# Turned tiles of a hybrid encoder layer: written to DRAM in four parts and read back in one transfer

## The chip, the cores and the metric

The kernel runs on one core of one Trainium2 chip. The core has five engines that run side by side: TensorE (PE in the profile, with its weight loads as PEld), VectorE (DVE), ScalarE (ACT), GpSimd (POOL) and SyncE (SP), which only issues transfers here. Sixteen DMA engines move the data. The metric is the device time of one execution in microseconds (us), the median of several runs.

## The reference

One layer of a bidirectional encoder, with 512 tokens of width 2048, all in float32:

```python
def hybrid_layer(x, norm_w, w_in, ...):
    h = rms_norm(x, norm_w)
    proj = jnp.einsum('bsd,de->bse', h, w_in)
    q, k, v, g_attn, xr, g_lru = jnp.split(proj, SPLITS, axis=-1)
    attn_out = attention_group(q, k, v, q_norm_w, k_norm_w)
    lru_out = lru_group(xr, conv_w, conv_b, lru_wa, lru_ba, lru_wx, lru_bx, lru_lambda)
    mixed = jnp.concatenate([rms_norm(attn_out, attn_norm_w) * jax.nn.silu(g_attn),
                             rms_norm(lru_out, lru_norm_w) * jax.nn.silu(g_lru)], axis=-1)
    return x + jnp.einsum('bse,ed->bsd', mixed, w_out)
```

The attention has 8 heads of 128 on 2 key/value heads, with a norm and a rotary embedding on queries and keys and a softmax over all 512 tokens. The other branch is a short convolution with a gated linear recurrence in both directions. `w_in` is 2048 x 4608 and `w_out` 2048 x 2048.

## The kernel before

**Products in three matmuls.** A float32 product is made of three matmuls on rounded operands (`mm3`, L152): each operand is split into a high part (a copy that rounds) and a low part (the difference), and high x high, high x low and low x high are added. So each weight tile `wr` passes ScalarE (`wh`, L223) and VectorE (`wl`, L224) before TensorE can use it, and so do x, keys, queries and attention weights. Weights come in chunks of 256 rows by 512 columns, 512 KB each, through a ring of three places.

**Turning tiles.** TensorE needs several tiles with rows and columns exchanged. Three kinds are turned without TensorE: the last three of the eight chunks of x (`TURNED = 5`), the keys and queries, and the attention weights (the softmax result, called p). VectorE turns every 32 x 32 block in place (`blocks`, L284, and the transpose at L713). What then remains is to bring each block to its new group of 32 partitions (`B = 32`, four groups, `NQ = 4`). That goes through a buffer in DRAM: a write of the whole tile, 128 partitions with 4 KB each (`put_aside`, L291; the first lines of `moved`, L718), and four reads back, one for each group of 32 partitions, which pick four pieces of 1 KB for every partition (`bring_back`, L297; the loop in `moved`). All of these transfers are issued by SP. Each tile has a DRAM buffer to itself.

- x: `xchunk` (L308) for chunks 5, 6 and 7 loads, turns, puts aside (`xd`), brings back (`xu`), scales on ScalarE (L343) and splits (L344). The table `moves` (L1206) says at which step of the first projection each part is issued.
- Keys and queries: `sent` (L637) turns a pair of heads and puts it aside (`qd`), `landed` (L649) brings it back (`lq`), `split_head` (L655) splits it (L658). The keys are one tile, the queries four.
- Attention weights: `weights` (L698) makes p for one head and 128 queries and turns it. Two of these are a unit; `moved` (L718) writes a unit (`pd`, L721) and, when it is called again, reads it (`pt`, L728) and splits it on ScalarE (`ph`) and VectorE (`pl`, both L732). `values` (L735) multiplies with v once the two units of a head are there. In `attention` (L764) a unit is written one step after its second half was made and read two steps later, and the values of a head come `LATE = 3` steps after it (`BEGIN, STEPS, LATE = 11, 2, 3`).

**The order.** TensorE's order is written by hand for the whole program (L1160): the matmuls of one projection are woven with the small products of the stage before. SP's order is written by hand in the first projection (L1172 to L1245), in the attention stage (L1340) and in the last stage. ScalarE and VectorE follow a hand-written order only in the first part of the first projection (L1175 to L1235) and in the last stage; elsewhere a planner orders them, with priorities (`AHEAD = 600` is a high one) and a few fixed successions (`behind`, `issue_after`). SP takes its instructions one after the other, so a transfer that has to wait holds all that stand behind it.

**Stages in time.** First projection with the start of x, to 54 us; recurrence woven with the second projection and keys and values, to 196; queries, to 262; attention woven with the gates, to 420; last gates and the output projection, to the end.

Of the kernel before, what the change touches and what calls it, by code (L numbers as in the profile page):

```python
# [11 lines left out]
F32 = mybir.dt.float32  # L12
# [5 lines left out]
P = 128  # L18
SEQ = 512
DM = 2048  # L20
KT = DM // P
NT = SEQ // P
HD = 128
NH = 8
# [24 lines left out]
H = 256  # L49


B = 32
TURNED = 5
NQ = P // B
# [9 lines left out]
def hybrid_kernel(  # L64
# [20 lines left out]
    nc = tc.nc  # L85
# [28 lines left out]
    dram = ctx.enter_context(tc.tile_pool(name="dram", bufs=1, space=bass.MemoryType.DRAM))  # L114
# [3 lines left out]
    def nm(s):  # L118
        cnt[0] += 1
        return f"{s}_{cnt[0]}"  # L120

    def x2():
        return pools["xw"].tile([P, SEQ], F32R, tag="x2", bufs=32, name=nm("x2"))
# [7 lines left out]
    def at(tag, bufs, shape, dt=F32):  # L131
        return pools["att"].tile([P, *shape], dt, tag=tag, bufs=bufs, name=nm(tag))
# [16 lines left out]
    def f(ap):  # L149
        return ap.bitcast(F32)  # L150
# [88 lines left out]
    def xload(c, nk=1):  # L239

        xc = b4(shape=(P, NT, 2 * P))
        for k in range(nk):
            ks = slice(k * 2 * P // nk, (k + 1) * 2 * P // nk)
            cs = slice(c * 2 * P + ks.start, c * 2 * P + ks.stop)
            nc.sync.dma_start(xc[:, :, ks], xf[:, cs].rearrange("(t p) d -> p t d", p=P))
            yield xc

    def behind(those):
        stack = ExitStack()
        for ins in those:  # L250
            stack.enter_context(tc.issue_after(ins))
        return stack

    def xturn(xc, kk, then=None):
        pt = mm()
        for t in range(NT):
            ks = slice(kk % 2 * P, (kk % 2 + 1) * P)
            nc.tensor.transpose(pt[:, t * P : (t + 1) * P], xc[:, t, ks], ident)  # L258
        if then:
            then()  # L260
        xh[kk], xl[kk] = x2(), x2()
        with behind(split_done[-1] if kk > 3 else ()):
            highs[kk // 2] = nc.scalar.activation(
                xh[kk], pt, AF.Identity, scale=nw[:, kk : kk + 1]
            ).ins
        nc.vector.scalar_tensor_tensor(
            xl[kk], pt, nw[:, kk : kk + 1], f(xh[kk]), op0=ALU.mult, op1=ALU.subtract
        )

    def xsquare(xc, c):  # L270
        for t in range(NT):
            if c >= TURNED:
                nc.scalar.activation(
                    xc[:, t, :], xc[:, t, :], AF.Square, accum_out=ssq[:, t, c : c + 1]
                )
                continue
            square = nc.vector.scalar_tensor_tensor(
                xc[:, t, :], xc[:, t, :], 1.0, xc[:, t, :], op0=ALU.mult, op1=ALU.mult,
                accum_out=ssq[:, t, c : c + 1],
            )  # L280
            if c == 1:
                squared.append(square.ins)

    def blocks(u, t, src):  # L284

        nc.vector.transpose(
            u[:, :, :, t, :].rearrange("p b k r -> p k b r"),
            src.rearrange("p (k b c) -> p k b c", k=2, c=B),
        )

    def put_aside(u, tag, bufs):  # L291

        aside_ = dram.tile([P, NQ, 2 * SEQ // NQ], F32, name=nm(tag), tag=tag, bufs=bufs)
        nc.sync.dma_start(aside_, u.rearrange("p b k t r -> p b (k t r)"))
        return aside_

    def bring_back(to, aside_):  # L297

        src = aside_.rearrange("(i c) b x -> b c i x", c=B)
        for b in range(NQ):  # L300
            nc.sync.dma_start(
                to[b * B : (b + 1) * B].rearrange("p i k t r -> p i (k t r)"), src[b]
            )

    def in_order(v):
        return v.rearrange("p (t i r) -> p i t r", t=NT, i=NQ)

    def xchunk(c):  # L308
        with tc.high_priority(AHEAD):
            (xc,) = xload(c)  # L310
        yield
        if c < TURNED:
            with tc.high_priority(AHEAD):
                for k in range(2):
                    xturn(xc, 2 * c + k)
            if c == 2:
                yield
            with behind(split_done[2][1:] if c == 2 else ()):
                xsquare(xc, c)
            yield  # L320
            return
        u, back = (
            ring.tile([P, NQ, 2, NT, B], F32, name=nm("xu")) for ring in (aring, hring)
        )
        with tc.high_priority(AHEAD), tc.issue_after(squared[-1] if c == TURNED else split_done[3][1]):
            for t in range(NT):
                blocks(u, t, xc[:, t, :])
        yield
        with tc.high_priority(AHEAD):
            there = put_aside(u, "xd", KT // 2 - TURNED)  # L330
        with tc.issue_after(highs[TURNED - 1]):
            xsquare(xc, c)
        yield
        with tc.high_priority(AHEAD):
            bring_back(back, there)
        yield
        with tc.high_priority(AHEAD), behind(split_done[-1]):
            for k in range(2):
                kk = 2 * c + k
                xh[kk], xl[kk] = x2(), x2()  # L340
                hi, lo = (in_order(v) for v in (xh[kk], xl[kk]))
                v = back[:, :, k]
                nc.scalar.activation(v, v, AF.Identity, scale=nw[:, kk : kk + 1])  # L343
                x_parts[:] = nc.scalar.copy(hi, v).ins, nc.vector.tensor_sub(lo, v, f(hi)).ins  # L344
        yield
# [289 lines left out]
    asides = []  # L635

    def sent(es, nh, *us):  # L637

        us = us or [
            pools["rot"].tile([P, NQ, 2, NT, B], F32, tag="uq", bufs=2, name=nm("uq"))  # L640
            for _ in range(nh // 2)
        ]
        for n, u in enumerate(us):
            for t, e in enumerate(es):
                blocks(u, t, e[:, 2 * n : 2 * n + 2].rearrange("p h d -> p (h d)"))
            yield
            asides.append(put_aside(u, "qd", 5))

    def landed(aside_):  # L649

        to = pools["qkv"].tile([P, NQ, 2, NT, B], F32, tag="lq", bufs=2, name=nm("lq"))
        bring_back(to, aside_)
        return to

    def split_head(pair, k, hi, lo):  # L655
# [4 lines left out]
    def kv(es):  # L660
        turned_k = sent(norm_rope(es, NKV, rk), NKV)
        yield 20
        opened("wx", "right")
        for t in range(NT):
            vv = es[t][:, NKV * HD :]
            vt = pools["qkv"].tile([P, 2, NKV * HD], F32R, tag="v", bufs=NT, name=nm("v"))
            vh[t], vl[t] = vt[:, 0, :], vt[:, 1, :]
            nc.scalar.copy(vh[t], vv)
            nc.vector.tensor_sub(vl[t], vv, f(vh[t]))
        yield from lru_squares()  # L670
        yield 2
        drain(turned_k)
        yield 6
        pair = landed(asides.pop(0))
        for h in range(NKV):
            yield (12, 4)[h]
            kt = pools["qkv"].tile([P, 2, SEQ], F32R, tag="kt", bufs=NKV, name=nm("kt"))
            kth[h], ktl[h] = kt[:, 0, :], kt[:, 1, :]
            those = split_head(pair, h, kth[h], ktl[h])
        parts = halved(  # L680
            sums["l"],
            lambda: pools["rope"].tile([P, SEQ], F32R, tag="kv", bufs=NT, name=nm("kv")),
            those,
        )
        yield 4
        spread(gbc, parts, NB * P)
# [30 lines left out]

    def moved(turned_, half, his):  # L718

        aside_ = dram.tile([P, NQ, NT * H // NQ], F32, name=nm("pd"), tag="pd", bufs=2 * NH)  # L720
        nc.sync.dma_start(aside_, turned_.rearrange("p a s t c -> p a (s t c)"))  # L721
        yield
        if half == 0:
            his += [at(n, 1, (NT, 2, NQ, H // NQ), F32R) for n in ("ph", "pl")]
        pt = at("pt", 2, (NQ, NT, H // NQ))
        src = aside_.rearrange("(i r) a x -> a r i x", r=B)
        for a in range(NQ):
            nc.sync.dma_start(  # L728
                pt[a * B : (a + 1) * B].rearrange("p i s x -> p i (s x)"), src[a]
            )  # L730
        hi, lo = (v[:, :, half].rearrange("p s i x -> p i s x") for v in his[:2])
        his += [nc.scalar.copy(hi, pt).ins, nc.vector.tensor_sub(lo, pt, f(hi)).ins]  # L732
        yield
# [27 lines left out]
    def next_pair():  # L761
        pairs.append(landed(asides.pop(0)))
# [415 lines left out]
    with tc.high_priority():  # L1178
# [13 lines left out]
        busy(WARM2)  # L1192
    stats = xstats()
    chunks = [xchunk(c) for c in range(1, KT // 2)]

    raws = {}
# [26 lines left out]
    for step in proj_feat(C_XR, a1, first, given):  # L1223
# [8 lines left out]
        c, e = step  # L1232
# [227 lines left out]
```

## Time and profile before

| what | value |
|---|---|
| median of 3 runs | 626.28 us (626.09 to 626.36) |
| the profiled execution, its own time | 626.48 us |
| its span, first to last instruction | 624.7 us |
| granted TensorE clock | 1.0 in every stage |
| ScalarE's wait for the reads of x (L343) | 5.9 us, 3 times |
| ScalarE's wait for the reads of attention weights (L732) | 3.4 us, 2 times |
| SP's wait for VectorE ahead of the writes of attention weights (L721) | 63.4 us, 15 times |
| HBM traffic over the span | 237 GB/s |

The span is what the trace covers; the time of a run also holds what lies before the first and after the last instruction. In the groups of the profile, a row names line, engine, operation, the tile written and the tiles read, then how often, the busy time, the mean time of one, and the idle time of the engine ahead of it with what ended it. In a timeline a row begins with the start in us and the duration. For a DMA the duration of an SP instruction is the issue alone; the landing is told apart from it. Matmuls overlap: one starts every 0.227 us or so while each is shown with 0.39.

### The profile page before, as it was taken

How to read it: one execution, taken by the hardware profiler on the slowest of the kernel's cores; microseconds unless marked ns; L12 is line 12 of the kernel's file. 1: busy time of each engine (PE TensorE's matmuls, PEld its weight loads, DVE VectorE, ACT ScalarE, POOL GpSimd, SP SyncE). 2: the span in 40 equal slices, each digit the busy share in tenths (PEclk: the TensorE clock that was granted, in tenths of full speed). 3: DMA queues.
4: the chain of work that ended last, by engine and by line, in shares of the span. 5: the costliest groups of instructions: out<-in, count | busy, mean ns of one | idle time of the engine just before them, and what ended most of it. 6: DMA issues, size and time to landing. Idle time of an engine off the chain costs nothing.

```text
span 624.7 us, 8293 instructions
## 1 busy us (share of the span) xinstructions
PE 620.0 (99%) x2756; PEld 512.6 (82%) x2756; DVE 495.3 (79%) x800; ACT 352.4 (56%) x617; POOL 101.8 (16%) x135
## 2 busy tenths in 40 slices
PE   9999999999999999999999999999999999999997
PEld 7888888888888888888888888888888888888886
DVE  5958979986699876887887888549979866887776
ACT  3675799479946833545485548338345633443441
POOL 0000210112003622622123223100210101010010
PEclk9999999999999999999999999999999999999999
DMA  8878686759774599479659646932995777897252
GB/s 285 277 210 271 178 202 171 175 135 195 239 235 137 170 247 240 100 204 270 192 173 258 201 137 192 256 91 76 283 254 184 216 250 242 288 333 230 68 202 101
DMA packets 74026, 127.61 MB, mean 204 GB/s; under 512 B 6664, under 2 KB 29312, under 8 KB 73984
## 3 DMA queue, kind: packets, MB, share of 16 engines
q1 hardware_dynamic: 66096, 109.65, 56.7%
q0 software_dynamic: 7712, 17.31, 14.3%
q8 instruction: 21, 0.34, 0.2%
q14 instruction: 21, 0.17, 0.1%
q10 hardware_dynamic: 176, 0.14, 0.1%
HBM read 110.29 MB, written 37.75 MB: 237 GB/s over the span
## 4 chain that ended last, share of the span: by engine, by line
PE 99%; DVE 0%; issue 0%
PE pj L154 20%; PE pj L155 20%; PE pj L153 20%; PE mm L1040 14%; PE pj L1040 11%; PE mm L155 4%; PE mm L154 3%; PE mm L153 3%; PE pj L394 2%; PE mm L258 1%; PE mm L1167 1%; PE mm L836 0%; DVE cb L1069 0%; PE mm L194 0%; PE mm L373 0%; DVE ones L159 0%
## 5 line engine op out<-in xcount | busy, mean ns | idle before, releaser
L153 PE MATMUL pj<-x,wh 128*128 128x512 f32 x368 | 143.5, 390 | 0.0
L155 PE MATMUL pj<-x,wl 128*128 128x512 f32 x368 | 143.2, 389 | 0.0
L154 PE MATMUL pj<-x,wh 128*128 128x512 f32 x368 | 143.2, 389 | 0.0
L223 ACT CAST wh<-wr 128x512 fp32r<-128x512 f32 x142 | 84.5, 618 | 81.5 <-PE pj L154 29.8
L224 DVE TENSOR_TENSOR wl<-wr,wh 128x512 fp32r<-128x512 f32 x144 | 98.5, 712 | 20.5 <-ACT wh L223 19.2
L888 ACT CAST wh<-wr 128x1024 fp32r<-128x1024 f32 (+1 forms) x72 | 60.6, 860 | 75.3 <-PE mm L1040 36.0
L889 DVE TENSOR_TENSOR wl<-wr,wh 128x1024 fp32r<-128x1024 f32 (+1 forms) x72 | 68.6, 983 | 29.0 <-ACT wh L888 28.9
L153 PEld LDWEIGHTS pj<-x,wh 128*128 128x128 f32 x368 | 69.1, 188 | 14.4
L154 PEld LDWEIGHTS pj<-x,wh 128*128 128x128 f32 x368 | 69.1, 188 | 14.3
L155 PEld LDWEIGHTS pj<-x,wl 128*128 128x128 f32 x368 | 69.1, 188 | 14.3
L154 PE MATMUL pj<-wl,x 128*128 128x512 f32 x192 | 74.7, 389 | 0.0
L155 PE MATMUL pj<-wh,x 128*128 128x512 f32 x192 | 74.7, 389 | 0.0
L153 PE MATMUL pj<-wh,x 128*128 128x512 f32 x192 | 74.7, 389 | 0.0
L912 POOL DMA_DIRECT2D t<-in_w_out_dram x40 | 33.6, 907 | 156.0 <-DMA t<-in_w_out_dram 96.9
L1040 PE MATMUL mm<-wh,ml 128*128 128x512 f32 x126 | 49.0, 389 | 0.0
L1040 PE MATMUL mm<-wh,mh 128*128 128x512 f32 x126 | 49.0, 389 | 0.0
L1040 PE MATMUL mm<-wl,mh 128*128 128x512 f32 x126 | 49.0, 389 | 0.0
L153 PEld LDWEIGHTS pj<-wh,x 128*128 128x128 f32 x192 | 36.0, 188 | 7.6
L154 PEld LDWEIGHTS pj<-wl,x 128*128 128x128 f32 x192 | 36.0, 188 | 7.5
L155 PEld LDWEIGHTS pj<-wh,x 128*128 128x128 f32 x192 | 36.0, 188 | 7.4
L712 POOL TENSOR_SCALAR p<-p,sm 128x512 f32<-128x512 f32 x32 | 24.2, 761 | 89.4 <-DVE sm L711 89.4
L1040 PE MATMUL pj<-wl,mh 128*128 128x512 f32 (+1 forms) x100 | 38.5, 385 | 0.0
(205 smaller groups left out, 1052.9 us busy)
## 6 DMA issues: line engine op xcount, KB each, us to landing
wr<-in_w_in_dram SPq DMA_DIRECT2D x71, 512.0 KB, 5.0
wr<-in_w_out_dram SPq DMA_DIRECT2D x21, 512.0 KB, 5.1
t<-in_w_out_dram POOLq DMA_DIRECT2D x40, 256.0 KB, 7.1
wr<-t SPq DMA_DIRECT2D x40, 256.0 KB, 5.8
pd<-u SPq DMA_DIRECT2D x16, 512.0 KB, 3.0
pt<-pd SPq DMA_DIRECT2D x64, 128.0 KB, 4.1
t<-in_w_out_dram SPq DMA_DIRECT2D x24, 256.0 KB, 5.3
wr<-in_w_out_dram SPq DMA_DIRECT2D x22, 256.0 KB, 4.2
```

The lines of the kernel that those rows point to most:

```text
L153: nc.tensor.matmul(acc, lh, rh, start=start, stop=False)
L154: nc.tensor.matmul(acc, lh, rl, start=False, stop=False)
L155: nc.tensor.matmul(acc, ll, rh, start=False, stop=stop)
L223: copy(hi, raw[:, k, :]).ins,
L224: nc.vector.tensor_sub(lo, raw[:, k, :], f(hi)).ins,
L258: nc.tensor.transpose(pt[:, t * P : (t + 1) * P], xc[:, t, ks], ident)
L394: nc.tensor.matmul(acc[e], w[:, e * P : (e + 1) * P], x_[2 * c + k], start=c == k == j == 0, stop=False,)
L712: last_pool[0] = nc.gpsimd.tensor_scalar(p, p, sm, 0.0, op0=ALU.mult, op1=ALU.add).ins
L888: nc.scalar.copy(hi[:, to], b)
L889: nc.vector.tensor_sub(lo[:, to], b, f(hi[:, to]))
L912: nc.gpsimd.dma_start(dst, src, accum_op=ALU.add)
L1040: nc.tensor.matmul(dst[s][:, es], lh[:, ts_], rh[:, es], start=i == ends_[0] and j == 0, stop=i == ends_[1] and j == 2,)
```

## The change

The roles of write and read are exchanged. Each turned tile is now written in four transfers, one for each group of 32 partitions, and each puts its pieces of 1 KB at once to the place in DRAM where the finished tile has them. The buffer then holds the finished tile, 128 rows of 4 KB, and one transfer reads it back. The read has to wait for all four writes. Where the writes and the reads are called from, the priorities, the number of buffers and all arithmetic stay as they are.

```diff
-    def put_aside(u, tag, bufs):
-
-        aside_ = dram.tile([P, NQ, 2 * SEQ // NQ], F32, name=nm(tag), tag=tag, bufs=bufs)
-        nc.sync.dma_start(aside_, u.rearrange("p b k t r -> p b (k t r)"))
+    def put_apart(u, tag, bufs):
+
+        aside_ = dram.tile([NQ, B, NQ, 2 * SEQ // NQ], F32, name=nm(tag), tag=tag, bufs=bufs)
+        for i in range(NQ):
+            nc.sync.dma_start(
+                aside_[:, :, i].rearrange("b c x -> c b x"),
+                u[i * B : (i + 1) * B].rearrange("p b k t r -> p b (k t r)"),
+            )
         return aside_
 
-    def bring_back(to, aside_):
-
-        src = aside_.rearrange("(i c) b x -> b c i x", c=B)
-        for b in range(NQ):
-            nc.sync.dma_start(
-                to[b * B : (b + 1) * B].rearrange("p i k t r -> p i (k t r)"), src[b]
-            )
+    def bring_whole(to, aside_):
+        nc.sync.dma_start(
+            to.rearrange("p i k t r -> p (i k t r)"), aside_.rearrange("b c i x -> (b c) (i x)")
+        )
...
     def moved(turned_, half, his):
 
-        aside_ = dram.tile([P, NQ, NT * H // NQ], F32, name=nm("pd"), tag="pd", bufs=2 * NH)
-        nc.sync.dma_start(aside_, turned_.rearrange("p a s t c -> p a (s t c)"))
+        aside_ = dram.tile([NQ, B, NQ, NT * H // NQ], F32, name=nm("pd"), tag="pd", bufs=2 * NH)
+        for i in range(NQ):
+            nc.sync.dma_start(
+                aside_[:, :, i].rearrange("a r x -> r a x"),
+                turned_[i * B : (i + 1) * B].rearrange("p a s t c -> p a (s t c)"),
+            )
         yield
         if half == 0:
             his += [at(n, 1, (NT, 2, NQ, H // NQ), F32R) for n in ("ph", "pl")]
         pt = at("pt", 2, (NQ, NT, H // NQ))
-        src = aside_.rearrange("(i r) a x -> a r i x", r=B)
-        for a in range(NQ):
-            nc.sync.dma_start(
-                pt[a * B : (a + 1) * B].rearrange("p i s x -> p i (s x)"), src[a]
-            )
+        nc.sync.dma_start(
+            pt.rearrange("p i s x -> p (i s x)"), aside_.rearrange("a r i x -> (a r) (i x)")
+        )
```

In `xchunk`, `sent` and `landed` the two helpers are replaced by the new ones, with nothing else changed.

More of the change, by code (lines that the diff above doesn't have):

```diff
@@ L329, in xchunk @@
         with tc.high_priority(AHEAD):
-            there = put_aside(u, "xd", KT // 2 - TURNED)
+            there = put_apart(u, "xd", KT // 2 - TURNED)
         with tc.issue_after(highs[TURNED - 1]):
@@ L334, in xchunk @@
         with tc.high_priority(AHEAD):
-            bring_back(back, there)
+            bring_whole(back, there)
         yield
@@ L646, in sent @@
             yield
-            asides.append(put_aside(u, "qd", 5))
+            asides.append(put_apart(u, "qd", 5))
     def landed(aside_):
         to = pools["qkv"].tile([P, NQ, 2, NT, B], F32, tag="lq", bufs=2, name=nm("lq"))
-        bring_back(to, aside_)
+        bring_whole(to, aside_)
         return to
```

## The prediction

> **What bounds the kernel now.** I read the page's busy times and its chain first, then TensorE's waits.
>
> ```profile
> span 624.7 us, 8293 instructions
> PE 620.0 (99%) x2756; PEld 512.6 (82%) x2756; DVE 495.3 (79%) x800; ACT 352.4 (56%) x617; POOL 101.8 (16%) x135
> PE 99%; DVE 0%; issue 0%
> PE mm L1167 <- DVE ones L159: 1.0, 1, 1.0
> ```
>
> TensorE is busy 620.0 of 624.7 us, the chain is TensorE's own for 99%, and its only recorded wait is 1.0 us for the constants at the very start. Everything in this change happens between 17 and 400 us. What the change gains there can only shorten waits that TensorE does not have; what it loses counts only once it makes TensorE wait, and then it counts in full, because no later gap can swallow it. So the question is not how long the transfers take but how much room they have.
>
> The transfers themselves, from the page's list of DMA issues:
>
> ```profile
> wr<-in_w_in_dram SPq DMA_DIRECT2D x71, 512.0 KB, 5.0
> pd<-u SPq DMA_DIRECT2D x16, 512.0 KB, 3.0
> pt<-pd SPq DMA_DIRECT2D x64, 128.0 KB, 4.1
> lq<-qd SPq DMA_DIRECT2D x20, 128.0 KB, 4.4
> xd<-xu SPq DMA_DIRECT2D x3, 512.0 KB
> xu<-xd SPq DMA_DIRECT2D x12, 128.0 KB, 3.7
> qd<-uq SPq DMA_DIRECT2D x3, 512.0 KB, 6.2
> qd<-u SPq DMA_DIRECT2D x2, 512.0 KB, 5.1
> ```
>
> 24 turned tiles (16 + 3 + 3 + 2 writes) go out in one transfer each and come back in four (64 + 20 + 12 = 96 reads).
>
> **The change part by part.** It adds 72 issues (24 x 3 more writes) and removes 72 (24 x 3 fewer reads): 120 before and after, the same bytes, and by the diff the 1 KB pieces move from the reading side to the writing side. SP's total work is unchanged; what moves is order. Before, the short part (one write) comes first and the long part (four reads) last; after it is the reverse.
>
> Attention, with sixteen of the 24. SP's order there is written by hand: the write of one unit, then at once the read of the unit before, then perhaps a pair of queries and a weight load. The rows of two units where the time is short:
>
> ```profile
> 322.72 0.34 SPq L721 DMA_DIRECT2D pd<-u  x1
> 323.16 2.17 SPq L728 DMA_DIRECT2D pt<-pd  x4
> 329.57 1.05 ACT L732 CAST ph<-pt 128x1024 fp32r<-128x1024 f32 x1
> 331.70 1.18 DVE L732 TENSOR_TENSOR pl<-pt,ph 128x1024 fp32r<-128x1024 f32 x1
> 333.09 0.39 PE L154 MATMUL mm<-pl,v 128*128 128x512 f32 x1
> 388.65 0.34 SPq L721 DMA_DIRECT2D pd<-u  x1
> 389.10 2.22 SPq L728 DMA_DIRECT2D pt<-pd  x4
> 395.31 1.05 ACT L732 CAST ph<-pt 128x1024 fp32r<-128x1024 f32 x1 [2.66 <-DMA pt<-pd]
> 396.39 1.23 DVE L732 TENSOR_TENSOR pl<-pt,ph 128x1024 fp32r<-128x1024 f32 x1 [2.14 <-ACT ph L732]
> 399.08 0.39 PE L154 MATMUL mm<-pl,v 128*128 128x512 f32 x1
> DMA to landing us min/median/max: 4.3/4.9/8.2
> ```
>
> In the second unit ScalarE waits 2.66 us for the read, so the read lands at 395.3; VectorE ends at 397.62 and TensorE takes the result at 399.08: 1.46 us of room. In the first, VectorE ends at 332.88 and TensorE takes it at 333.09: 0.21 us of room, but there ScalarE ends at 330.62 and VectorE starts only at 331.70, so the read has 1.29 us (1.08 + 0.21).
>
> After the change, the four writes take 4 issues. Bounds for one: 0.34 us (the whole write) and 0.55 (2.22 / 4, reads of the same 32-partition shape). I take 0.45, near the median of the reads: 1.8 us for four, between 1.4 and 2.2. Then comes one read of 512 KB. The trace has none of this shape; nearest are the weight loads of the same size in this stage, 4.3 to 8.2 us, median 4.9 (the last row of the fence, 20 weight loads issued from 270 to 420 us). I take 4.9, and keep 4.3 and 8.2 as ends. First unit: 322.72 + 1.8 + 0.1 + 4.9 = 329.5, against ScalarE's start at 329.57: no loss. Second: 388.65 + 6.8 = 395.45, against 395.3 now: 0.15 later, in 1.46 of room. Sum of both: 0. The room is gone at a landing of 6.2 us in the first and 6.2 in the second.
>
> [...]
>
> The start, with three tiles. SP, ScalarE, VectorE and TensorE around the second of them:
>
> ```profile
> 26.18 1.76 SPq L301 DMA_DIRECT2D xu<-xd  x4
> 28.52 1.26 SPq L294 DMA_DIRECT2D xd<-xu  x2
> 34.15 1.74 SPq L301 DMA_DIRECT2D xu<-xd  x4
> SPq L301 <- DMA xd<-xu: 9.8, 2, 5.5
> 35.99 0.40 SPq L211 DMA_DIRECT2D wr<-in_w_in_dram  x1
> 36.49 1.83 SPq L301 DMA_DIRECT2D xu<-xd  x4
> 42.50 0.31 SPq L185 DMA_DIRECT2D vec_st<-in_lru_bx_dram  x1
> SPq L185 <- DMA wr<-in_w_in_dram: 2.9, 1, 2.9
> 39.31 1.34 ACT L343 ACTIVATE xu<-xu,nw 128x512 f32<-128x512 f32 x2 [2.98 <-DMA xu<-xd]
> 42.41 1.28 DVE L224 TENSOR_TENSOR wl<-wr,wh 128x512 fp32r<-128x512 f32 x2
> 43.54 0.39 PE L155 MATMUL pj<-x,wl 128*128 128x512 f32 x1
> ```
>
> The tile lands at 39.3 and ScalarE waits for it; the chain through the split of x and then of the weights ends its first half at 43.05 (42.41 + 0.64), and TensorE uses it at 43.54: 0.49 us of room. One more thing is visible: the load of a bias vector waits 2.9 us for a weight transfer that has nothing to do with it. That transfer (35.99) is eight issues ahead of it (itself, four reads, three vector loads). So SP waits for the eighth issue back to land. With 4 + 1 issues in another order this counts: between 26 and 34 us SP now issues one read, one weight load, eight writes, so the seventh write waits for the read and the eighth for the weight load.
>
> Step by step: the read at 26.18 takes 0.45 instead of 1.76, the weight load behind it goes at 26.7 and lands 5.0 later (the median of the list), 31.7; the first four writes go from about 27.2 to 29.0, the last of the other four at 31.7. Now the first write lands 5.6 us after its issue (28.52 to 34.15, where SP's wait for it ends); in four parts it lands between 32.8 (5.6 after the first part) and 34.2 (5.6 after the last). The read goes then and lands 4.9 later, 37.7 to 39.1, against 39.3 now. So the room grows from 0.49 to between 0.7 and 2.1 us; TensorE did not wait here, so this gains 0. At the other end, a read of 8.2 us lands at 41.0 to 42.4 and costs up to 2.6 us, once.
>
> [...]
>
> Keys and queries, five tiles, planned by the scheduler:
>
> ```profile
> 226.81 0.69 DVE L830 TENSOR_TENSOR kv<-hsum,kv 64x512 fp32r<-64x512 f32 x1
> L836 PE MATMUL mm<-kv,ones_r x1: 397/397/397, 236.6 to 236.6; 128*128 128x512 f32 x1
> ```
>
> The chain behind the keys ends at 227.5 on VectorE and TensorE wants it at 236.6: 9.1 us of room, more than the whole difference between the two orders (0.15 and the ends 8.2 - 4.9 = 3.3). I cost these at 0.
>
> Sum: 0 of 624.7 us. The profiled execution took 626.48 us, 1.78 more than its span; the median of the runs is 626.28, 0.20 lower. My forecast is **626.3 us**. A measurement of this kernel can tell about 0.2% (1.25 us) from no change.
>
> **The rivals.** First, *another plan on ScalarE and VectorE*. In attention only TensorE and SP have an order by hand; the other two are ordered by a planner that sees other transfers now. For it: the room of 0.21 us at 333.09. An instruction put in front of VectorE's step costs 0.64 to 1.28 us (the two or one of the split rows at 42.41), so 0.4 to 1.1 us of waiting for a head. At four of eight heads by the middle, 0.75, it is 3.0 us: 629.3. Against it: everything planned keeps the same inputs and priorities, and the reads shift by 0.15 us.
>
> Second, *the single read lands late*: this is the case that ends slower by the transfers themselves. Place: the read behind the four writes in attention. It decides from a landing of 6.2 us; at 8.2 both units above wait 2.0, 4.0 us together: 630.3. For it: ScalarE already waits at 395.31, so there every microsecond is passed on. Against it: the median of 4.9, and the four reads it replaces took 6.2 from first issue to landing (389.10 to 395.3).
>
> Third, *the four writes wait for one another*, because their pieces interleave in one buffer. Each part then costs a landing of 3.0 us:
>
> ```profile
> L721 SPq DMA_DIRECT2D pd<-u x16: 319/338/344, 274.7 to 393.7; - x16
> 620.83 0.38 ACTq L1064 DMA_DIRECT2D out_dram<-cb  x1
> L1064 SPq DMA_DIRECT2D out_dram<-cb x4: 332/332/333, 618.3 to 621.5; - x4
> DMA to landing us min/median/max: 2.5/3.6/8.1
> ```
>
> Units come every 7.9 us ((393.7 - 274.7) / 15); SP would need 3 x 3.0 + 0.45 + 0.45 + 0.4 = 10.3, 2.4 too many, 38 us over sixteen units: about 664. Against it: the two halves of the last output rows, interleaved in the same way, go out at 620.83 and 621.5, 0.7 us apart, while no output lands in under 2.5.
>
> Fourth, *faster*: the room of the start turns into time. TensorE would have to wait there now, and it doesn't; 625.0 at the best if the profile hides small waits.
>
> **How the numbers follow.** Forecast 0.67; another plan 0.15; late read 0.10; the start's late read (2.6 us) 0.02; writes in series 0.03; faster 0.03. Slower by over 0.2% is 0.15 + 0.10 + 0.02 + 0.03 = 0.30, within 0.67, faster 0.03. Range 625.7 to 629.8: it holds the forecast, the first rival to past its middle and the beginning of the second; outside remain the rest of these two (some 0.11), the series (0.03) and faster (0.03).
>
> **What would show it.** Right: 120 issues of the turned tiles, DMA packets and those under 2 KB as before, TensorE's only wait that at L1167, and the end of its work at the same place. The read of one unit issued about 1.9 us after the first of the four writes, landing about 4.9 us later. In the start the second read issued at 33 to 34 and ScalarE's L343 earlier than 39.31. Wrong: a wait of TensorE at the matmuls on ph or pl (first two rivals, told apart by whether ScalarE waits for pt), SP waiting at the second write of a tile for the first (third), or an eighth issue back that lands late and holds a weight load.

## The result, and the profile after

The changed kernel takes 630.12 us (median; 628.51 to 630.18), the kernel before 626.32 us beside it: a ratio of 1.0054, with a 95% interval from 1.0041 to 1.0067. It is slower by about 3.8 us. The profiled execution took 630.08 us, with a span of 628.3.

The page of the changed kernel, in the lines that answer to those shown of before:

```profile
span 628.3 us, 8246 instructions
PE 621.7 (99%) x2756; PEld 513.3 (82%) x2756; DVE 496.1 (79%) x800; ACT 353.3 (56%) x617; POOL 103.6 (16%) x135
PE   9999999999999999999899999999999999999997
PEclk9999999999999999999899999999999999999999
DMA packets 74026, 127.61 MB, mean 203 GB/s; under 512 B 6664, under 2 KB 29312, under 8 KB 73984
pd<-u SPq DMA_DIRECT2D x64, 128.0 KB, 2.9
pt<-pd SPq DMA_DIRECT2D x16, 512.0 KB, 4.8
```

The transfers are as the diff says: 64 writes of 128 KB and 16 reads of 512 KB, with as many packets as before. The loss has one place. TensorE's row and the row of its granted clock both show an 8 in the 20th slice of 40 (298 to 314 us); the clock's row has no other. TensorE's waits (engine, line and what it waited for: us in total, times, longest) name what is late there:

```profile
PE mm L154 <- DVE pl L735: 1.6, 1, 1.6
PE mm L1170 <- DVE ones L159: 1.0, 1, 1.0
PE mm L153 <- ACT ph L735: 0.2, 1, 0.2
```

The wait at L1170 is the old one at L1167. The other two are one event, at the values of the first head. In the timeline of the changed kernel (start, duration, engine, line, operation, and in brackets the idle time before):

```profile
299.70 0.39 PE L155 MATMUL mm<-kt,q 128*128 128x512 f32 x1
300.34 0.50 PE L153 MATMUL mm<-ph,v 128*128 128x512 f32 x1 [0.25 <-ACT ph L735]
302.45 0.80 PE L154 MATMUL mm<-pl,v 128*128 128x512 f32 x1 [1.60 <-DVE pl L735]
303.04 0.63 PE L155 MATMUL mm<-ph,v 128*128 128x512 f32 x1
303.47 0.63 PE L153 MATMUL mm<-ph,v 128*128 128x512 f32 x1
```

Read the starts, not the idle times: matmuls start 0.227 us apart where nothing is wrong, and here the distances are 0.64 and 2.11. That is 0.41 + 1.88 of waiting. From 302.45 they are 0.59 and 0.43 apart although nothing is waited for. The windows of one microsecond say why (time; busy time of PE, PEld, DVE, ACT, POOL with counts; then the granted clock, the DMA share and GB/s):

```profile
302.00:303.00 1.00, 0.55 (x1) 0.50 (x2) 1.00 (x3) 0.00 (x0) 0.00 (x0) 0.64 0.07 27
303.00:304.00 1.00, 1.00 (x4) 0.77 (x3) 1.00 (x2) 0.00 (x0) 0.00 (x0) 0.50 0.00 0
...
306.00:307.00 1.00, 1.00 (x6) 0.82 (x5) 0.91 (x2) 0.00 (x0) 0.73 (x2) 1.00 0.08 16
```

In the window at half clock 4 matmuls are busy, in the one at full clock 6. The clock falls to 0.50 after the wait and is back at 306: six distances of 0.427 and two that are only partly lengthened, one at each end, cost 0.26 + 6 x 0.20 + 0.05 = 1.5 us. The waiting is 0.41 + 1.88 + 0.11 = 2.4 us. The 0.11 lies in the distance behind 302.45: at full clock, in experiment 1 below, the first distance after such a wait is still 0.34 (300.64 to 300.98). Together that is 3.9 us, against 3.6 in the spans (628.3 - 624.7). The other 0.3 lies ahead of it: a matmul that started at 236.6 us in the kernel before starts at 236.3 in this execution, because the start, at 5 to 7 us, was shorter.

**What made pl late.** VectorE's timeline after:

```profile
293.52 0.71 DVE L714 STREAM_TRANSPOSE u<-p 128x512 f32<-128x512 f32 x1 [0.83 <-POOL p L713]
296.05 0.69 DVE L478 TENSOR_TENSOR ev<-pj,rbc 128x512 f32<-128x512 f32 x1 [1.82 <-PE pj L155]
296.66 1.22 DVE L735 TENSOR_TENSOR pl<-pt,ph 128x1024 fp32r<-128x1024 f32 x1
297.79 0.69 DVE L709 TENSOR_REDUCE mx<-mm 128x1 f32<-128x512 f32 x1
...
301.21 1.18 DVE L735 TENSOR_TENSOR pl<-pt,ph 128x1024 fp32r<-128x1024 f32 x1
```

and before:

```profile
292.02 1.21 DVE L732 TENSOR_TENSOR pl<-pt,ph 128x1024 fp32r<-128x1024 f32 x1
...
293.62 0.69 DVE L708 TENSOR_REDUCE mx<-mm 128x1 f32<-128x512 f32 x1 [0.32 <-PE mm L155]
...
296.87 0.68 DVE L477 TENSOR_TENSOR ev<-pj,rbc 128x512 f32<-128x512 f32 x1
...
298.09 1.18 DVE L732 TENSOR_TENSOR pl<-pt,ph 128x1024 fp32r<-128x1024 f32 x1
```

Before, the row maximum (mx) stood ahead of the first evacuation of the gate product (ev, `evac_bc`, L477). After, ev stands ahead of both pl and mx. It needs the last matmul of its product, which starts at 295.62 and ends at 296.01, and VectorE stands still for 1.82 us. Everything behind it is late: pl of the first half head, then mx at 297.79 in place of 293.62, then the exponential on ScalarE, then ph, then the second pl at 301.21 in place of 298.09. ScalarE's timeline shows the middle of that chain, first before and then after:

```profile
294.65 0.68 ACT L710 ACTIVATE p<-mm,mx 128x512 f32<-128x512 f32 x1
...
295.83 1.05 ACT L732 CAST ph<-pt 128x1024 fp32r<-128x1024 f32 x1
```

```profile
298.57 0.69 ACT L711 ACTIVATE p<-mm,mx 128x512 f32<-128x512 f32 x1 [3.43 <-DVE mx L709]
...
299.25 1.04 ACT L735 CAST ph<-pt 128x1024 fp32r<-128x1024 f32 x1
```

ScalarE waited 3.43 us for mx and then not at all for pt. So the read was not late; the split stood in a queue. In the traces the two programs have the same order on TensorE and GpSimd, and another one on SP (by the diff), VectorE and ScalarE (44 of 800 and 22 of 619 instructions stand elsewhere). Only the transfers differ between the two programs, so the planner ordered these two engines anew because of them.

### The profile page after: what moved, and what is told of

Its sections match the earlier page's. It is cut to its first block, busy times and chain, and to the rows that moved or that the text cites. A ratio compares the mean times of both kernels' runs of the same rounds, so it can differ in the third digit from the quotient of the medians.

```text
span 628.3 us, 8246 instructions
## 1 busy us (share of the span) xinstructions
PE 621.7 (99%) x2756; PEld 513.3 (82%) x2756; DVE 496.1 (79%) x800; ACT 353.3 (56%) x617; POOL 103.6 (16%) x135
## 4 chain that ended last, share of the span: by engine, by line
PE 94%; DVE 2%; DMA 1%; SPq 1%; issue 1%; POOL 0%; ACT 0%; DVEq 0%; ACTq 0%
PE pj L153 19%; PE pj L154 19%; PE pj L155 19%; PE mm L1043 14%; PE pj L1043 11%; PE mm L154 3%; PE mm L155 3%; PE mm L153 3%; PE pj L395 2%; PE mm L258 1%; DVE u L714 1%; DMA pd<-u 1%; DMA qd<-u 1%; PE mm L1170 1%; POOL p L713 0%
```

## The experiments

Theory A: the planned order of VectorE at the first gate product is the whole loss. Rival B: the new transfers cost something themselves (the joined read, or the four writes). Edits are against the changed kernel.

**1. The evacuation behind the row maximum.** All transfers stay as changed; the first ev of each gate product is fixed behind the last but two of the row maxima planned so far.

```diff
-    def evac_bc(acc, first=()):
+    def evac_bc(acc, first=(), those=()):
...
-                with behind(first if n else ()):
+                with behind(first if n else those):
...
-            nc.vector.tensor_reduce(mx, sc, axis=AX.X, op=ALU.max, negate=True)
+            maxes.append(
+                nc.vector.tensor_reduce(mx, sc, axis=AX.X, op=ALU.max, negate=True).ins
+            )
...
-            evacs = evac_bc(acc, summed)
+            evacs = evac_bc(acc, summed, maxes[-3:-2])
```

> The changed kernel with one instruction moved in VectorE's order: the first evacuation of a gate product (ev, which waits for TensorE's accumulation until 296.0 us) comes after the split of the first attention unit (pl) and the row maximum of the eighth score tile (mx) instead of ahead of them. All transfers stay as changed. Theory A (the loss is the place of this one waiting instruction): the maximum is done at about 296.1 instead of 298.5, the second unit's pl ends at 300.5 to 301.0 instead of 302.4, TensorE's wait shrinks from 2.7 us to between 0.3 and 0.9, its clock stays at 1.0, and the time is 626.3 to 627.2. Rival B (the loss is in the transfers, the joined read or the four writes landing late): nothing of the transfers is touched, so about 630 as in the changed kernel.

Measured: 627.07 us against 626.49 before, a ratio of 1.0008 (0.9999 to 1.0018). In the order that the two traces show, this ev is the only instruction of the whole program, on any engine, that stands elsewhere than in the changed kernel, and the loss is all but gone. VectorE's timeline and TensorE's in this run:

```profile
295.15 0.68 DVE L711 TENSOR_REDUCE mx<-mm 128x1 f32<-128x512 f32 x1
295.98 0.69 DVE L478 TENSOR_TENSOR ev<-pj,rbc 128x512 f32<-128x512 f32 x1
...
299.40 1.18 DVE L738 TENSOR_TENSOR pl<-pt,ph 128x1024 fp32r<-128x1024 f32 x1
```

```profile
300.64 0.50 PE L154 MATMUL mm<-pl,v 128*128 128x512 f32 x1 [0.40 <-DVE pl L738]
```

The second pl starts 1.8 us earlier than in the changed kernel but still 1.3 later than before, and TensorE still loses 0.67 us there (distances of 0.78 and 0.34). The clock stays at 1.0 (the mean is 1.000). That is what A had (0.3 to 0.9 us of waiting).

**2. Four reads in place of one.** Four writes as in the change, and four reads of 32 rows of 4 KB each.

```diff
-        nc.sync.dma_start(
-            pt.rearrange("p i s x -> p (i s x)"), aside_.rearrange("a r i x -> (a r) (i x)")
-        )
+        for a in range(NQ):
+            nc.sync.dma_start(
+                pt[a * B : (a + 1) * B].rearrange("p i s x -> p (i s x)"),
+                aside_[a].rearrange("r i x -> r (i x)"),
+            )
```

The reads of x, keys and queries are divided in the same way.

> Writes in four parts as changed, but the read split into four again, one for each group of 32 partitions, now of whole 4 KB rows. The plan on VectorE has ev ahead of pl and mx as in the changed kernel. A: the same wait of TensorE, 2 to 3 us at the values of the first head, and 628.3 to 630.3. B with the joined read as the cause: no wait, 626.3.

Measured: 634.32 us, a ratio of 1.0122 (1.0101 to 1.0143). If the joined read were what is dear, dividing it should have helped. It lost 7.8 us against the kernel before, 4 more than the changed kernel, and most of it has the same form. TensorE's waits on pl:

```profile
PE mm L154 <- DVE pl L739: 3.5, 3, 1.6
```

One of the three is that at 300 us, a small one is at 336 us, and the third, at 370 us, follows the first evacuation of the second gate product, with VectorE in the same succession:

```profile
365.35 0.69 DVE L480 TENSOR_TENSOR ev<-pj,rbc 128x512 f32<-128x512 f32 x1 [0.97 <-PE pj L155]
...
367.16 0.69 DVE L711 TENSOR_REDUCE mx<-mm 128x1 f32<-128x512 f32 x1
```

So A's mechanism holds, but not its size here: I had counted on one such place and the order of this kernel has two. The mean granted clock of this execution is 0.997, against 1.000 in the kernel before. No fixed succession holds these instructions apart at either place, and here the planner chose badly at both. Another 0.8 us is a wait at 7 us for a load of x, which no edit here touches; experiment 4's profile has 0.4 us of it.

**3 and 4. One half of the change at a time.** In the third kernel the attention weights alone go the new way (x, keys and queries as before); in the fourth x, keys and queries alone do (`moved` as before). Two places of the third kernel's edit:

```diff
-            there = put_apart(u, "xd", KT // 2 - TURNED)
+            there = put_aside(u, "xd", KT // 2 - TURNED)
...
-            bring_whole(back, there)
+            bring_back(back, there)
```

> The change made to the attention weights alone; x, keys and queries go as before. The plan puts pl ahead of ev here, but ev and two weight splits still ahead of mx. A: mx is done at about 298.7, the second unit's pl at 302 to 303, TensorE waits 2 to 3 us at the values of the first head; 628.3 to 630.5. B: also slower, since the attention transfers are the changed ones. This run tells whether the attention part is enough for the loss.

> The change made to x, keys and queries alone; the attention weights go out in one write and come back in four reads as before. The plan on VectorE at the first head is that of the changed kernel (ev, pl, mx). A: the same wait of TensorE at the values of the first head, 2 to 3 us, and 628.3 to 630.3, although no attention transfer of the weights was touched. B: the attention transfers are those of the kernel before, so 626.3.

Measured: 630.09 us for the attention weights alone (1.0051; 1.0036 to 1.0066) and 630.57 for the rest alone (1.0065; 1.0045 to 1.0084), 0.3 above what A had given for it. Either half costs as much as the whole, so it is not a price per transfer, which would add up. In the third, ev stands behind the first half's pl but still ahead of mx (296.56 and 298.37 us). The fourth kernel is the clearest witness: no transfer of the attention weights differs from before, and yet its VectorE shows the same rows:

```profile
296.14 0.69 DVE L478 TENSOR_TENSOR ev<-pj,rbc 128x512 f32<-128x512 f32 x1 [2.27 <-PE pj L155]
...
297.88 0.68 DVE L709 TENSOR_REDUCE mx<-mm 128x1 f32<-128x512 f32 x1
...
301.30 1.18 DVE L733 TENSOR_TENSOR pl<-pt,ph 128x1024 fp32r<-128x1024 f32 x1
```

**5. The evacuation behind a whole split, at the wrong head.** The first ev behind the last pl of a head whose two halves are both split (beside the other lines of experiment 1):

```diff
-            evacs = evac_bc(acc, summed)
+            done = [those[-1] for those in pts.values() if len(those) == 6]
+            evacs = evac_bc(acc, summed, done[:1] or maxes[-3:-2])
```

> The changed kernel with all its transfers, but VectorE's first evacuation of each gate product is put behind the whole split of the attention weights (the last pl of the head that is next). Theory A (VectorE's order at the first gate product is all of the loss): compared with the kernel that only puts the evacuation behind the row maximum, pl ends 0.15 + 0.69 us earlier (the evacuation's wait and its duration go), which is more than the 0.67 us that TensorE still waited there; no wait of TensorE at the values of the first head is left, and the time is 626.2 to 626.8, the same as before the change. Rival B (the new transfers cost something of their own, spread over the stages): 627 to 628 although the wait is gone. Rival C (a product's accumulator that is read out later holds TensorE instead): a new wait of TensorE at a matmul on pj for an ev, 0.5 us or more, and a time over 627.

Measured: 647.23 us, a ratio of 1.0332 (1.0315 to 1.0348). At this point the first head has already left `pts`, so the edge caught the head after it. What followed is rival C at full size, in VectorE's timeline and in TensorE's:

```profile
310.89 1.22 DVE L738 TENSOR_TENSOR pl<-pt,ph 128x1024 fp32r<-128x1024 f32 x1 [3.00 <-ACT ph L738]
312.04 2.48 DVE L478 TENSOR_TENSOR ev<-pj,rbc 128x512 f32<-128x512 f32 x4
```

```profile
304.00 0.39 PE L155 MATMUL pj<-x,wl 128*128 128x512 f32 x1
312.77 0.79 PE L153 MATMUL pj<-x,wh 128*128 128x512 f32 x1 [8.38 <-DVE ev L478]
```

TensorE can go on until 304.0 without the evacuation; then it has no accumulator for the next product. It waits so at both of the first two gate products, 16.1 us in all. The run shows what an evacuation may not do, and one more thing: with the evacuation out of the way until then, no wait at the values of the first head is left.

**6. The changed kernel again.**

> The changed kernel again, with nothing altered, for the spread of its times. If the second part of the loss is a fall of TensorE's clock to half after the one long wait, which some executions escape, the times fall into two groups, near 628.5 (wait alone, 2.4 to 2.7 us above TensorE's own work) and near 630.1 (wait and half clock), with nothing between. If the loss is something that grows smoothly (transfers that land at random), the times spread evenly between 627 and 631.

Measured: 628.36, 628.68, 628.92, 630.02, 630.60 and 630.62 us. With the four runs of the first comparison (628.51, 630.08, 630.16, 630.18) these are four below 629 and six above 630, and nothing in the 1.1 us between. The mean granted clock parts them without exception: 0.999 in the lower group, 0.996 or 0.997 in the upper. Within a group the times spread by 0.6 us, more than I had expected; the means, 628.6 and 630.3, are 1.7 apart, and the half clock in the profile above came to 1.5. (The kernel before, too, spreads beside these runs, from 626.0 to 627.9 us in eleven, but with the clock at 0.999 or 1.0 in all of them.) The profiled execution here, of 628.36 us, has the same wait (1.6 us for pl and 0.2 for ph among TensorE's waits, as in the profile above) and the full clock behind it:

```profile
303.00:304.00 1.00, 1.00 (x6) 0.82 (x5) 1.00 (x3) 0.00 (x0) 0.00 (x0) 1.00 0.00 0
```

**7. The evacuation behind the split of the right head.** The other three evacuations of a product already wait for the splits of the head that is used next (`summed`). Now the first does too:

```diff
-                with behind(first if n else ()):
+                with behind(first):
```

> The changed kernel with its transfers; now the first evacuation of each gate product waits, as the other three already do, for the two low parts of the head that is consumed next (and not for those of the head after it, as the last but one experiment had it by mistake). There pl of the first head ended at 300.06 with no wait of TensorE at its values, and TensorE ran on without the evacuation until 304.0. Theory A: no wait of TensorE at matmuls on ph, pl or pj, time 626.2 to 626.8, the time before the change. Rival B (the transfers have a price of their own): 627 to 628 with no such wait. Rival C (accumulators read out late): a wait at a matmul on pj of 0.5 us or more; by the 3.9 us between 300.1 and 304.0 it should not come.

Measured: 626.39 us against 626.50 before, a ratio of 0.9994 (0.9985 to 1.0003), with every transfer of the change in place. VectorE's timeline, TensorE's, and TensorE's only wait:

```profile
299.09 1.18 DVE L735 TENSOR_TENSOR pl<-pt,ph 128x1024 fp32r<-128x1024 f32 x1
300.20 1.88 DVE L478 TENSOR_TENSOR ev<-pj,rbc 128x512 f32<-128x512 f32 x3
```

```profile
300.41 0.39 PE L153 MATMUL mm<-ph,v 128*128 128x512 f32 x1
300.64 0.39 PE L154 MATMUL mm<-pl,v 128*128 128x512 f32 x1
```

```profile
PE mm L1170 <- DVE ones L159: 1.0, 1, 1.0
```

The evacuation now fills the time between 300.2 and 304.0, in which nobody waits for it. The transfers of the change cost nothing that these runs can tell from zero, and gain nothing: rival B falls. This edit was not tried on the kernel before, where TensorE has no wait that it could take away; and it moves more than one instruction (10 on VectorE, 5 on ScalarE and one on GpSimd against the changed kernel), so the single cause is shown by experiment 1, and the full time by this one.

## Why the prediction was right and wrong

**The likeliest case did not happen.** I forecast 626.3 us with 0.67 on no change, and the kernel is 3.8 us slower. The first rival, *another plan on ScalarE and VectorE*, is what happened; the time is 0.8 above the 629.3 that I gave for it, and 0.3 above the upper end of the range. That 629.3 came so near is luck: three heads too many in the price made up for a longer wait at the one and for a fall of the clock that was not in it.

**TensorE as the bound, and what follows from it: right.** The 3.8 us are TensorE's waits and its clock, in full, and no later gap swallowed them.

**The transfers of the attention weights: right, term by term.** The two units of the prediction in the timeline of the changed kernel, SP, ScalarE, VectorE and TensorE:

```profile
326.98 1.77 SPq L723 DMA_DIRECT2D pd<-u  x4
333.69 1.05 ACT L735 CAST ph<-pt 128x1024 fp32r<-128x1024 f32 x1 [1.35 <-DMA pt<-pd]
392.29 1.78 SPq L723 DMA_DIRECT2D pd<-u  x4
398.67 1.05 ACT L735 CAST ph<-pt 128x1024 fp32r<-128x1024 f32 x1 [2.41 <-DMA pt<-pd]
399.76 1.23 DVE L735 TENSOR_TENSOR pl<-pt,ph 128x1024 fp32r<-128x1024 f32 x1 [1.57 <-ACT ph L735]
402.69 0.39 PE L154 MATMUL mm<-pl,v 128*128 128x512 f32 x1
```

Four writes take 1.77 and 1.78 us to issue (1.8 predicted), and ScalarE has the tile 6.71 and 6.38 us after the first of them (6.8 predicted). The median landing of the read is 4.8 us (4.9 predicted from the weight loads). VectorE ends at 400.99 in the second, 1.70 us before TensorE's matmul at 402.69 (in the first it ends 0.69 before it): no loss at either.

**The start: the direction right, the size too small.** SP and ScalarE there, in the timeline:

```profile
32.40 0.34 SPq L302 DMA_DIRECT2D xu<-xd  x1
36.07 1.34 ACT L344 ACTIVATE xu<-xu,nw 128x512 f32<-128x512 f32 x2 [1.10 <-DMA xu<-xd]
```

and among SP's waits

```profile
SPq L295 <- DMA wr<-in_w_in_dram: 0.4, 1, 0.4
```

The second read goes at 32.4 (33 to 34 predicted), and ScalarE starts at 36.07 in place of 39.31, 3.2 us earlier where I had 0.2 to 1.6. The last of the eight writes did wait for the weight load eight issues back, 0.4 us. TensorE gained nothing from any of it, as the sum had it. Keys and queries: TensorE wants the sums at 236.3 (236.6 before) and does not wait, as predicted.

**The step that failed** is in the argument against the first rival: "everything planned keeps the same inputs and priorities, and the reads shift by 0.15 us". The same inputs and priorities did not give the same order. The planner exchanged an evacuation with a row maximum in a place where neither touches the new transfers, and it did so in all four kernels with other transfers that it was left to order by itself (the changed one and experiments 2 to 4). How it weighs a transfer, and so why it chose this, no run shows. With 0.15 I had the rival's chance too low: both halves of the change led to it by themselves.

**The price of that rival was mis-sized too.** I had 0.4 to 1.1 us of waiting at each of four heads, 3.0 together. It was one head of eight, with 2.4 us. The 0.64 to 1.28 us that I took were the duration of an instruction put ahead of pl. What counted was how long that instruction itself waits for its input (1.82 us), and that mx, ahead of the exponential and ph, is held as well. The rest, 1.5 us of half clock in six runs of ten, stands in no row of the kernel before, whose clock is 1.0 throughout.

**The other rivals.** *The single read lands late*: no. ScalarE waited 5.3 us for pt in three places and TensorE in none of them, and at the stall ScalarE waited for mx. *The four writes wait for one another*: no; those of the attention weights land in 2.9 us (median) and four are issued in 1.8. *Faster*: no; the start's 3.2 us met a TensorE that did not wait.

## What to carry to other kernels

Where a planner orders a queue, a change of transfers is also a change of every planned order, even stages away from the transfers: before pricing the transfers, list the places where an instruction that waits for something late could be put ahead of the chain that the bound engine waits for, and price each with that instruction's own wait. Compare the orders of all queues before and after, and when a loss has one place, restore the order there before blaming the transfer. An evacuation wants a fixed place on both sides: behind the chain it could hold (pl, at 300.2 us here) and ahead of the accumulator's next use (304.0).

## What the hardware showed beside this

A wait of TensorE of some 2 us (2.11 between two starts in the profile above) came with half clock behind it in one execution of the changed kernel and with the full clock in another. In the first, half clock lasted about 3.4 us (0.64, 0.50, 0.50 and 0.65 in the four windows from 302 to 306 us). The second, in experiment 6, has the same waits of TensorE at pl and ph (1.6 and 0.2 us) and 1.00 in every window from 299 to 307 us. So the length of the wait alone does not decide. By the mean clock six of the ten executions are like the first (0.996 or 0.997) and four like the second (0.999). A wait of 0.67 us left the clock at 1.0 (experiment 1, mean 1.000). Experiment 5, with two waits of 8.4 and 7.7 us, has a mean of 0.986. Around the end of the first of them, at 312.77 us, the clock is 0.50 in every window from 310 to 317 us, and the next two distances are 0.60 and 0.42 in place of 0.227; half of the 4.2 us from 312.77 to 317 is an estimate of about 2 us for the price of the half clock behind that wait. Why one execution falls and another doesn't, these runs do not settle.
